# A longer pad in front of the arenas: their tiles begin at residue 64 of 512 bytes instead of 96

## The chip, the cores and the metric

The kernel runs on one core of a Trainium2 chip (trn2). The metric is the device time of one execution in microseconds; the time quoted for a kernel is the median of its runs. TensorE (PE in the profile) multiplies, with its weight loads shown apart as PEld; ScalarE is ACT, VectorE is DVE, GpSimd is POOL, and SP issues most of the DMA transfers.

## The reference: what is computed

A trunk of two layers on 256 tokens with 1024 features, in float32. Each layer is a half-step SwiGLU FFN, a token mixer, and another half-step FFN; the mixer is stick-breaking attention in layer 0 and an RG-LRU recurrent block in layer 1. Each sub-layer reads an RMS norm of x that is shifted and scaled by a vector worked out from the conditioning c, and its result is gated before it is added to x.

```python
def sublayer_input(x, g, mod_j):
    shift, scale, gate = mod_j[:, 0], mod_j[:, 1], mod_j[:, 2]
    h = rmsnorm(x, g) * (1 + scale[:, None, :]) + shift[:, None, :]
    return h, (1 + gate)[:, None, :]

def swiglu(h, w_gu, w_down):
    g, u = jnp.split(h @ w_gu, 2, axis=-1)
    return (jax.nn.silu(g) * u) @ w_down
...
    for layer in range(DEPTH):
        mod = (c_act @ mod_w[layer] + mod_b[layer]).reshape(B, N_SUB, 3, D_MODEL)
        h, g = sublayer_input(x, norm_g[layer, 0], mod[:, 0])
        x = x + MACARON_W * g * swiglu(h, ffn_w_gu[layer, 0], ffn_w_down[layer, 0])
...
    return rmsnorm(x, final_norm_g)
```

The FFN is 2816 wide, the recurrent block 1280, and the attention has 16 heads of 64.

## The kernel before

**Layout.** Features lie on the 128 partitions and the 256 tokens along the free axis, so a chunk of 128 features of x is one tile of 256 columns. Every weight matrix is cut into pieces of 128x128.

**Two halves of a number.** A float32 product is made of three matmuls in the type fp32r: each operand is split into a rounded part and the rest, and the product is weights-high times data-high, weights-high times data-low, and weights-low times data-high. The weights are split on the way in: SP loads 1 MB into a buffer `raw`, ACT copies half of it into a buffer `wh` (L519), DVE subtracts to get `wl` (L522). So one 128x128 piece of weights costs three matmuls of 256 columns, all issued at L548 in `Acc.group`. The weights are the stationary operand, loaded 128 columns at a time, and the activations are the moving operand, 256 columns of 4 bytes or 1024 bytes in each partition.

**The stages.** An FFN has an *up* stage and a *down* stage. In the up stage the moving operand is `hx`, the 8 high and 8 low chunks of the normalised input, and each of the 22 pairs of gate and up tiles takes 48 matmuls. In the down stage (`down`) the moving operand is `arenar`, the 22 high and 22 low chunks of the activated result, and it takes 22 x 8 x 3 = 528 matmuls. The attention and the recurrent block end in a `down` of 8 x 8 x 3 = 192 such matmuls from their own arena. The first two tiles of a sub-layer after the first one run on 258 columns, on `hx` tiles that hold x times the scale (`up_first`), while the norm is still being worked out.

**Where tiles lie.** Most tiles are taken one after another from a pool `const`, in the order in which the program asks for them. Three pads shift what follows: `HXPAD` ahead of `hx`, `HKPAD` ahead of `hk`, `ARPAD` at the end of the pool, after the tables of modulation values. After it comes one small tile of 32 bytes (`mhalf`), and then the arenas: at the start of each sub-layer the function `enter` closes the previous arena and opens new ones, `arenar` of fp32r and `arenaf` of float32, at the same address each time.

```python
    whr, _ = ring("wh", 7, HALF, F32R)
    wlr, _ = ring("wl", 7, HALF, F32R)
    const.tile([P, HXPAD], F32, tag="pad0", name="pad0")
    hxr, _ = ring("hx", 20, TX, F32R, pitch=320)
    const.tile([P, HKPAD], F32, tag="pad2", name="pad2")
    hkr, _ = ring("hk", 2, T, F32R)
...
    fixed("pad1", ARPAD)
```

The addresses that the built program gives to its tiles, as residues of 512 bytes within a partition, are these. All pieces of `wh` and `wl` begin at 128 (a piece is 512 bytes long). The `hx` tiles are 1280 bytes apart and begin at 64 and 320 in turn; the high part of a chunk mostly has the one and the low part the other. `hk`, a copy of the first chunk of `hx`, begins at 128. An arena is handed out in cells of 512 bytes, so every tile in it begins at one residue, which is 96.

**Two kinds of interruption.** In the up stages, the tiles numbered 2, 3, 7, 9, 11, 15 and 19 (`KICKS`) read `hk` instead of the first chunk of `hx`: the same numbers at another residue. In `down`, `kick_op` (L734) puts one bf16 matmul of 64 columns with zero weights behind the first three matmuls of a chosen chunk (`kicks`): chunk 0 in an FFN, chunk 1 in the two mixers.

**What sets the order.** The program records every operation with an estimated cost and sorts them by a list scheduler (`Program.schedule`); the instructions of each engine then run in the order found. The scheduler knows buffers by their cells and not by their addresses in bytes.

Of the kernel before, what the change touches and what calls it, by code (L numbers as in the profile page):

```python
# [32 lines left out]
NFIRST = 2  # L33
LAT0, RATE0, RATE = 950.0, 390.0, 360.0
SMALL = (0, 7)
HXPAD, HKPAD, ARPAD = 112, 16, 64
KICKS = (2, 3, 7, 9, 11, 15, 19)

OFF_NG = 0
# [1282 lines left out]
```

## Time and profile before

| | |
|---|---|
| runs | 979.4, 979.3 and 978.39 us, median 979.3 us |
| profiled execution, from its first to its last instruction (span) | 978.6 us; no other time of it is given |
| TensorE matmuls and weight loads | 8102 of each |
| VectorE busy | 799.1 us |
| ScalarE busy | 564.4 us |
| read from memory | 248.92 MB, 255 GB/s over the span |
| mean granted TensorE clock | 0.997 |

The page of the profile is a page of one execution. "Busy" is the time in which an engine had an instruction under way. Matmuls are pipelined: a row gives one 256-column matmul about 0.28 us, but the next one starts after less than half of that, so what a stage costs is read from the distance between starts, and not from the duration of one. In the view in order of time, a row stands for one or more equal instructions that follow each other: "x2" at 620.46 and the row after it at 620.68 are three matmuls, and the next three begin at 620.80. The view of stretches gives for each stretch its length, the busy time of each engine with the number of instructions that are under way in it, the granted clock, and what the DMA engines did.

### The profile page before, as it was taken

What the parts mean: (1) busy time and instruction counts of PE and PEld (TensorE: products, weight loads), DVE (VectorE), ACT (ScalarE), POOL (GpSimd) and SP (SyncE); (2) the same over time, 40 slices, a digit from 0 to 9 for tenths busy, and PEclk for the clock granted to TensorE, in tenths of its full rate; (3) what the DMA queues carried; (4) which work ended last, traced back from release to release, by engine and by line L of the source; (5) the groups of instructions that cost most, each with busy time, mean ns of one, the idle gap of its engine ahead of it and who ended that gap; (6) DMA issues with size and microseconds to landing.
All of it is one profiled execution on the core that took longest, in us unless ns stands there. A gap on an engine that the chain in (4) does not pass through costs nothing.

```text
span 978.6 us, 19751 instructions
## 1 busy us (share of the span) xinstructions
PE 960.4 (98%) x8102; PEld 948.4 (97%) x8102; DVE 799.1 (82%) x1325; ACT 564.4 (58%) x907; POOL 3.9 (0%) x16
## 2 busy tenths in 40 slices
PE   7999999999999999999999999999999999999996
PEld 5999999999999999999999999999999999999996
DVE  7999898798998999998789999835997996555443
ACT  4475544378886854454367544534879785444333
POOL 0000000000000000000000000000000000000000
PEclk9999999999999999999999999999999999999998
DMA  8999899854666489999977999855243646555521
GB/s 313 330 345 362 330 367 349 326 210 154 255 217 219 161 322 373 356 344 341 347 268 266 351 367 349 320 194 191 86 173 129 259 172 237 195 192 196 173 86 44
DMA packets 48189, 251.25 MB, mean 257 GB/s; under 512 B 5473, under 2 KB 6369, under 8 KB 28386
## 3 DMA queue, kind: packets, MB, share of 16 engines
q1 hardware_dynamic: 47378, 249.30, 69.6%
q8 instruction: 63, 1.03, 0.4%
q10 hardware_dynamic: 720, 0.69, 0.2%
q14 instruction: 28, 0.23, 0.1%
HBM read 248.92 MB, written 1.05 MB: 255 GB/s over the span
## 4 chain that ended last, share of the span: by engine, by line
PE 88%; DVE 6%; DMA 3%; ACT 2%; issue 1%; SPq 0%; DVEq 0%; ACTq 0%
PE bank L548 82%; DMA raw<-in_gu 3%; PE bank L880 2%; DVE wl L522 2%; DVE arenaf L1059 1%; PE bank L1003 1%; ACT arenaf L498 1%; PE bank L565 1%; DVE rawm L580 1%; ACT wh L519 1%; PE bank L956 1%; PE bank L981 1%; DVE arenaf L1056 0%; PE bank L624 0%; PE bank L983 0%
## 5 line engine op out<-in xcount | busy, mean ns | idle before, releaser
L548 PE MATMUL bank<-hx,wh 128*128 128x256 f32 (+1 forms) x3236 | 563.9, 279 | 4.5 <-ACT hx L498 2.9
L519 ACT ACTIVATE wh<-raw 128x1024 fp32r<-128x1024 f32 (+1 forms) x328 | 337.2, 1047 | 313.8 <-PE bank L548 221.7
L548 PEld LDWEIGHTS bank<-hx,wh 128*128 128x128 f32 x3236 | 492.8, 189 | 6.9 <-ACT hx L498 3.8
L522 DVE TENSOR_TENSOR wl<-raw,wh 128x1024 fp32r<-128x1024 f32 (+1 forms) x328 | 389.5, 1208 | 111.7 <-ACT wh L519 110.6
L548 PE MATMUL bank<-hx,wl 128*128 128x256 f32 (+1 forms) x1618 | 449.8, 278 | 0.0
L548 PEld LDWEIGHTS bank<-hx,wl 128*128 128x128 f32 x1618 | 305.5, 189 | 0.0
L548 PE MATMUL bank<-arenar,wh 128*128 128x256 f32 x1664 | 297.1, 282 | 0.0
L548 PEld LDWEIGHTS bank<-arenar,wh 128*128 128x128 f32 x1664 | 255.2, 188 | 0.1
L548 PE MATMUL bank<-arenar,wl 128*128 128x256 f32 x832 | 233.7, 281 | 0.0
L580 DVE SCALAR_TENSOR_TENSOR rawm<-rawm,cact 128x1024 f32<-128x1024 f32 x143 | 174.1, 1221 | 24.1 <-DMA rawm<-in_modw 23.4
L548 PEld LDWEIGHTS bank<-arenar,wl 128*128 128x128 f32 x832 | 156.8, 188 | 0.0
L498 ACT ACTIVATE arenar<-a 128x256 fp32r<-128x256 f32 x88 | 35.7, 407 | 8.6 <-DVE a L767 8.3
L772 DVE TENSOR_TENSOR arenar<-a,arenar 128x256 fp32r<-128x256 f32 x88 | 36.6, 419 | 0.6 <-ACT arenar L498 0.5
L767 DVE TENSOR_TENSOR a<-bank,sg 128x256 f32<-128x256 f32 x82 | 34.1, 418 | 0.5 <-ACT sg L498 0.3
L548 PE MATMUL bank<-hk,wh 128*128 128x256 f32 x156 | 31.2, 291 | 0.0
L498 ACT ACTIVATE sg<-bank 128x256 f32<-128x256 f32 x82 | 29.7, 367 | 1.4 <-PE bank L548 1.4
L498 ACT ACTIVATE hx<-x,mf 128x256 fp32r<-128x256 f32 x40 | 18.8, 504 | 19.5 <-DVE x L689 19.5
L498 ACT ACTIVATE hx<-hpre,mf 128x256 fp32r<-128x256 f32 x48 | 23.5, 503 | 10.8 <-DVE hpre L650 8.2
L689 DVE SCALAR_TENSOR_TENSOR x<-bank,mf,x 128x256 f32<-128x256 f32 x48 | 21.7, 479 | 9.8 <-PE bank L548 9.6
L548 PEld LDWEIGHTS bank<-hk,wh 128*128 128x128 f32 x156 | 24.0, 189 | 0.5
L880 PE MATMUL bank<-wh,hx 128*128 128x256 f32 x128 | 23.4, 280 | 0.0
L652 DVE SCALAR_TENSOR_TENSOR hx<-hpre,mf,hx 128x256 fp32r<-128x256 f32 x48 | 23.0, 480 | 0.5 <-ACT hx L498 0.5
(109 smaller groups left out, 541.6 us busy)
## 6 DMA issues: line engine op xcount, KB each, us to landing
raw<-in_gu SPq DMA_DIRECT2D x79, 1024.0 KB, 6.0
rawm<-in_modw SPq DMA_DIRECT2D x144, 512.0 KB, 6.7
raw<-in_wdn SPq DMA_DIRECT2D x44, 1024.0 KB, 6.4
raw<-in_win SPq DMA_DIRECT2D x10, 1024.0 KB, 4.9
raw<-in_qk SPq DMA_DIRECT2D x8, 1024.0 KB, 4.9
raw<-in_gu SPq DMA_DIRECT2D x14, 512.0 KB, 7.5
raw<-in_wout SPq DMA_DIRECT2D x5, 1024.0 KB, 5.2
raw<-in_wv SPq DMA_DIRECT2D x4, 1024.0 KB, 6.6
```

The costliest lines, as they stand in the source:

```text
L498: act.activation(o(), i(), f, **{k: (v() if callable(v) else v) for k, v in kw.items()})
L519: act.activation(h()[:, :m], raw()[:, a : a + m], AF.Copy)
L522: dve.tensor_tensor(lo()[:, :m], raw()[:, a : a + m], f32(h()[:, :m]), ALU.subtract)
L548: pe.matmul(o(b()), wc(u()), xc(v()), start=start and n == 0, stop=stop and n == len(passes) - 1, skip_group_check=True)
L565: pr.op("PE", c_mm(n, 4), lambda: pe.matmul(o(b()), wc(w()), xc(x32()), start=start, stop=stop, skip_group_check=True), [w, x32] + ([] if ...
L580: dve.scalar_tensor_tensor(raw(), raw(), 1.0, cact(), ALU.mult, ALU.mult, accum_out=m()[:, t : t + 1])
L652: V(lambda: dve.scalar_tensor_tensor(lo()[:, :T], hp(), sh()[:, c], f32(hi()[:, :T]), ALU.add, ALU.subtract), T, [hp, (sh, d), hi], [lo], ...
L689: dve.scalar_tensor_tensor(x[d](), acc.b()[:, j * T : (j + 1) * T], gate()[:, d : d + 1], x[d](), ALU.mult, ALU.add)
L767: V(lambda: dve.tensor_tensor(a(), b()[:, T:], sg(), ALU.mult), T, [(b, (1, 0)), sg], [a])
L772: V(lambda: dve.tensor_tensor(y[1](), a(), f32(y[0]()), ALU.subtract), n, [a, y[0]], [y[1]])
L880: pe.matmul(o, u()[:, tb * P : (tb + 1) * P], v()[:, c0 : c0 + 256], start=start and n == 0, stop=k == KD - 1 and n == 2, skip_group_check ...
L956: pe.matmul(zb[e]()[:, BL[i]], v()[rows, kc], w()[rows, qc], start=False, stop=i == 1 and n == 2, skip_group_check=True)
```

## The change

One number changes. The pad tile `pad1` is 184 floats long instead of 64, so 736 bytes of each partition instead of 256. `mhalf` and all arenas move up by 480 bytes; the arenas begin at residue 64 of 512 bytes instead of 96, and `mhalf` at 32 instead of 64. Nothing else moves: `raw`, `wh`, `wl`, `hx`, `hk`, x and all the tables keep their addresses. The instructions and their order are the same on every engine in both programs (5497 rows on TensorE, 1122 on VectorE, 853 on ScalarE, 20 on GpSimd and 323 on SyncE, row by row); only addresses within them differ.

```diff
-HXPAD, HKPAD, ARPAD = 112, 16, 64
+HXPAD, HKPAD, ARPAD = 112, 16, 184
```

## The prediction, made before the changed kernel ran

> **What bounds the kernel now.** The first view is the page: the busy row, the granted clock by slices and the engine shares of the chain that ended last.
>
> ```profile
> span 978.6 us, 19751 instructions
> PE 960.4 (98%) x8102; PEld 948.4 (97%) x8102; DVE 799.1 (82%) x1325; ACT 564.4 (58%) x907; POOL 3.9 (0%) x16
> ...
> PEclk9999999999999999999999999999999999999998
> ...
> PE 88%; DVE 6%; DMA 3%; ACT 2%; issue 1%; SPq 0%; DVEq 0%; ACTq 0%
> ```
>
> TensorE is under way for 98% of the span at full clock, and 88% of the chain runs through it. So the second question is whether it waits inside its stages. The view of waits, TensorE alone, gives in its longest row (microseconds in total, times, longest)
>
> ```profile
> PE bank L548 <- ACT hx L498: 2.9, 2, 2.6
> ```
>
> and the others are shorter still. For most of the span the kernel therefore lasts as long as its matmuls take one after the other, and a nanosecond on the distance between starts counts in full. The third view, the groups of instructions with their shapes apart, says how many matmuls read the arenas.
>
> ```profile
> L548 PE MATMUL bank<-hx,wh 128*128 128x256 f32 x2916 | 504.6, 278 | 4.5 <-ACT hx L498 2.9 <-DVE hx L652 1.4
> ...
> L548 PE MATMUL bank<-arenar,wh 128*128 128x256 f32 x1664 | 297.1, 282 | 0.0
> ...
> L548 PE MATMUL bank<-arenar,wl 128*128 128x256 f32 x832 | 233.7, 281 | 0.0
> ```
>
> 1664 + 832 = 2496 matmuls take an arena tile as moving operand: 4 x 528 in the FFNs' down stages and 2 x 192 in the mixers'. They stand beside 2916 and more on `hx` of the same shape, with weights in the same buffers at the same residue, 128. What differs is the residue of the moving tile: 96 for the arenas, 64 and 320 for `hx`.
>
> The fourth view, the order of time on TensorE, compares the distances. Below are the first and the last row of three pieces of 17 threes (51 matmuls) each, and nothing else runs on TensorE between them.
>
> ```profile
> 620.46 0.39 PE L548 MATMUL bank<-hx,wh 128*128 128x256 f32 x2
> ...
> 626.24 0.39 PE L548 MATMUL bank<-hx,wh 128*128 128x256 f32 x2
> ```
>
> ```profile
> 59.78 0.40 PE L548 MATMUL bank<-hx,wh 128*128 128x256 f32 x2
> ...
> 65.79 0.40 PE L548 MATMUL bank<-hx,wh 128*128 128x256 f32 x2
> ```
>
> ```profile
> 659.00 0.40 PE L548 MATMUL bank<-arenar,wh 128*128 128x256 f32 x2
> ...
> 665.03 0.40 PE L548 MATMUL bank<-arenar,wh 128*128 128x256 f32 x2
> ```
>
> 5.78, 6.01 and 6.03 us, so 113.3, 117.8 and 118.2 ns per matmul. The reader is to see two things. The same instruction on `hx` runs at two paces, and keeps to either for tens of matmuls; I call them the **fast lock** (113.3) and the **slow lock** (117.8). And the arenas at residue 96 run at neither but slightly behind the slow one. That this holds for whole stages is shown by the view of stretches, from the matmul behind the bf16 one of L734 to the end of each FFN's down stage, with the recurrent block's as fourth row:
>
> ```profile
> core 0: us, PE busy (x) PEld busy (x) DVE busy (x) ACT busy (x) POOL busy (x), PEclk, DMA share, GB/s
> ...
> 141.69:203.90 62.21, 62.21 (x527) 62.21 (x527) 52.39 (x85) 26.93 (x43) 0.00 (x0) 1.00 0.90 336
> 443.56:505.78 62.22, 62.22 (x528) 62.22 (x527) 50.71 (x81) 25.80 (x36) 0.00 (x0) 1.00 0.94 340
> 627.31:689.53 62.22, 62.22 (x529) 62.22 (x527) 31.61 (x43) 26.15 (x36) 0.00 (x0) 1.00 0.53 185
> 762.01:784.47 22.46, 22.46 (x193) 22.46 (x192) 21.42 (x42) 15.91 (x32) 0.00 (x0) 1.00 0.65 249
> 905.96:968.17 62.21, 62.21 (x527) 62.21 (x527) 24.89 (x30) 23.32 (x32) 0.00 (x0) 1.00 0.30 102
> ```
>
> 62.2 us for the 525 matmuls that are left in each (2 to 4 more are still under way at the edges), 118.5 ns each with the 0.09 us that the L734 matmul costs its successor. It is the same at 94% and at 30% DMA share, so it isn't traffic; the arena stages have one pace of their own.
>
> **The change, part by part.**
>
> *Matmuls that read the arenas as moving operand.* After the change their tiles begin at 64 with weights still at 128, which is what two of three matmuls on `hx` have (the middle one reads the low part, at 320, 256 bytes further). So the trace shows their pace: one of the two locks. By the fast one each saves (6.03 - 5.78) / 51 = 4.9 ns. Which lock is the open point. The first of the three pieces is the end of an up stage, 0.7 us ahead of its down stage, so `down` is entered in the fast lock, but then L734 interrupts the stream after three matmuls and the lock is drawn again. Here are four such draws on `hx` at 64: a short stall at 58.92, a longer one at 52.96, a restart behind L956 at 287.60, and at 70.39 six matmuls on `hk`.
>
> ```profile
> 58.92 0.55 PE L548 MATMUL bank<-hx,wh 128*128 128x256 f32 x2
> ...
> 59.43 0.40 PE L548 MATMUL bank<-hx,wh 128*128 128x256 f32 x2
> ```
>
> ```profile
> 53.83 0.39 PE L548 MATMUL bank<-hx,wh 128*128 128x256 f32 x2
> ...
> 54.16 0.39 PE L548 MATMUL bank<-hx,wh 128*128 128x256 f32 x2
> ```
>
> ```profile
> 288.05 0.39 PE L548 MATMUL bank<-hx,wh 128*128 128x256 f32 x2
> ...
> 288.38 0.39 PE L548 MATMUL bank<-hx,wh 128*128 128x256 f32 x2
> ```
>
> ```profile
> 70.39 0.40 PE L548 MATMUL bank<-hk,wh 128*128 128x256 f32 x2
> ...
> 71.81 0.39 PE L548 MATMUL bank<-hx,wh 128*128 128x256 f32 x2
> ...
> 73.17 0.39 PE L548 MATMUL bank<-hx,wh 128*128 128x256 f32 x2
> ```
>
> The first falls into the slow lock (0.35 to 0.36 us for three, as the piece from 59.78 goes on), the second and third into the fast one (0.33 to 0.34), the fourth leaves the slow for the fast (four threes in 1.36 us). The fast is the likelier outcome. What L734 does to a stream at 64 no row shows; the nearest row is its present effect on a stream at 96:
>
> ```profile
> 627.27 0.20 PE L734 MATMUL bank<-ident,zero 128*128 128x64 bf16 x1
> 627.31 0.49 PE L548 MATMUL bank<-arenar,wh 128*128 128x256 f32 x2
> ...
> 627.75 0.40 PE L548 MATMUL bank<-arenar,wh 128*128 128x256 f32 x2
> ```
>
> One long first matmul (0.49 us for two against 0.40), like a restart after a stall. So I take the restarts' odds, two of three for the fast lock, raised a little because the entry is in it. All four FFN stages meet L734 in the same position behind the same three matmuls, so they fall alike.
>
> The sum for the fast lock: FFNs 4 x 525 x 4.9 ns = 10.3 us; recurrent block 189 x 4.9 = 0.9 us; attention, whose 192 are cut into pieces by other products, some two thirds in the fast lock, 0.6 us. Together **11.8 us**, less some 8 matmuls of settling per stage, 6 x 8 x 4.9 ns = 0.2 us: **11.6 us**.
>
> *Matmuls that read an arena in another way.* Scores, sums and values of the attention have both operands in the arena or weights elsewhere, and the 72 single-pass pieces on float32 read `arenaf`. The pitch between moving and weight tiles inside one arena stays, so I take nothing; the bound, 4.9 ns on some 300 such instructions either way, is 1.5 us, and half of that lies beside ScalarE and VectorE work on the chain.
>
> *Reads and writes of the arenas by ScalarE and VectorE.* The rows for 256 columns at different residues:
>
> ```profile
> L772 DVE TENSOR_TENSOR arenar<-a,arenar 128x256 fp32r<-128x256 f32 x88 | 36.6, 419 | 0.6 <-ACT arenar L498 0.5
> L498 ACT ACTIVATE arenar<-a 128x256 fp32r<-128x256 f32 x88 | 35.7, 407 | 8.6 <-DVE a L767 8.3
> ...
> L498 ACT ACTIVATE sq<-x 128x256 f32<-128x256 f32 x45 | 17.2, 406 | 2.9 <-DVE x L689 2.3 <-DVE ssq L617 0.5
> L617 DVE TENSOR_TENSOR ssq<-ssq,sq 128x256 f32<-128x256 f32 x40 | 16.8, 421 | 2.6 <-ACT sq L498 1.4
> ```
>
> 419 and 421, 407 and 406 ns, with the arena at 96 and `ssq` and `sq` at 128: no effect of the residue, taken as zero.
>
> *What is late next.* A down stage of 62.2 us would last 59.6 and asks for its weights and modulation tiles sooner. In the stretch from 443.56 that is 340 GB/s x 62.2 us = 21.1 MB in 59.6 us, 355 GB/s. The stretch
>
> ```profile
> 75.00:81.00 6.00, 6.00 (x56) 6.00 (x55) 6.00 (x8) 4.15 (x6) 0.00 (x0) 1.00 1.02 372
> ```
>
> shows 372, by which the load takes 56.9 us, so it still fits. If only 345 were had, it would last 61.3 us, and 1.7 us of the gain would go in this stage and about 1 us in the first, where 336 GB/s stand. I charge 0.2 us in all. The forecast is 978.6 - 11.4 = 967.2 us for the profiled execution; the median of the runs is 0.7 us above its span, so **967.9 us**.
>
> **A rule that speaks against the change.** The Trainium skill, SBUF — State Buffer, section "Who interferes with whom", has one cause of contention alone, the port pair shared by VectorE and GpSimd, and says "PE and ACT never wait on anyone"; TensorE: Matmul & The Clock Gate, "Step-by-step: what each phase is for", adds that loading the next weights takes no read bandwidth from the running matmul. By these an address can't matter, and the sum would be zero, 979.3 us. The trace doesn't bear this out as it stands: one instruction shape runs at 113.3, 117.8 and 118.2 ns with full clock and no wait.
>
> **The rivals.**
>
> *The slow lock* (nothing that can be measured). L734 leaves the stream at 117.8 ns: 2496 x 0.4 ns = 1.0 us saved, 978.3 us. For it: the draw at 58.92. Against it: the other three, and the entry in the fast lock. The case in which the residue is not the cause at all, and `hx` is faster for another reason (its order of output banks, its pitch), is as likely to end here, at 979.3.
>
> *Mixed.* The mixers or some stages keep to the slow lock: with two of four FFN stages 973 us. For it: the pieces of the attention are redrawn often. Against it: the four stages start alike. A DMA bound that gives back 2.7 us (above) ends at about 970.5.
>
> *Slower: no lock, with 64 after 64.* On `hx` the low part lies at 320; in the arena both parts lie at 64, and nothing in the trace has that. A stream of 64s that doesn't lock has a row: the `hx` matmuls of 258 columns,
>
> ```profile
> 515.88 0.28 PE L548 MATMUL bank<-hx,wl 128*128 128x258 f32 x1
> ...
> 517.69 0.28 PE L548 MATMUL bank<-hx,wl 128*128 128x258 f32 x1
> ```
>
> 15 matmuls in 1.81 us, 120.7 ns, and 119.8 ns without their two extra columns at 113.3 / 256 ns each. That is 1.6 ns above today's pace, 2496 x 1.6 = 4.0 us, **983.3 us**. It decides if the step of 256 bytes between high and low part matters; against it speaks that in the fast lock two tiles at 64 also follow each other, the third of a group and the first of the next, and the rows still come every 0.34 us.
>
> **How the numbers follow.** Fast lock in all or nearly all stages 0.68, own range 966 to 970 (all 2496 at 4.9 ns and 0.8 us for the other products below; a DMA bound of 2 us above). Mixed 0.10, 970 to 977. Slow lock or no effect 0.15, around 978.3 to 979.3. Slower 0.07. To leave out no more than 2 in 10 the range has to take in the slow lock's nearest part: 965.8 to 978.3. A measurement of this kernel can tell about 0.2% (2 us) from no change, so faster means below 977.3: 0.78; same 0.15; slower 0.07.
>
> **What would show it.** Right: threes 0.34 us apart in the four stages behind L734, stretches of 59.6 us, and the up stages unchanged at 113.3. Slow lock: threes an even 0.353 us apart. Slower: threes of uneven length above 0.355. A DMA bound would show as waits of L548 for ACT or DVE in the stages from 141 and 443. The prediction is wrong if L734 starts a stream at 64 in the slow lock, or if the pace is set by something other than the moving tile's residue.

## The result, and the profile after

| | before | changed kernel | ratio, 95% interval |
|---|---|---|---|
| first comparison | 979.35 us (978.39 to 979.92, 4 runs) | 970.06 us (968.3 to 973.06, 4 runs) | 0.9913 (0.989 to 0.9937) |
| repeated later (experiment 5) | 979.02 us (977.7 to 980.01, 7 runs) | 967.38 us (967.06 to 967.7, 4 runs) | 0.9883 (0.9868 to 0.9898) |

The kernel became faster by 9.3 us, and by 11.6 us when it was measured again; the forecast was 967.9 us. The execution profiled in the first comparison is the longest of its four, 973.06 us with a span of 971.4 us, so its trace shows both the gain and where part of it went.

The page of this execution, with the busy row and the chain that ended last:

```profile
span 971.4 us, 19751 instructions
PE 951.9 (98%) x8102; PEld 938.5 (97%) x8102; DVE 797.0 (82%) x1325; ACT 562.7 (58%) x907; POOL 3.8 (0%) x16
...
PE 79%; DVE 8%; DMA 8%; ACT 3%; issue 2%; SPq 0%; DVEq 0%; ACTq 0%
```

The counts are those of before, and TensorE is still under way for 98% of the span, with 8.5 us less. But its share of the chain fell from 88% to 79%, and that of DMA rose from 3% to 8%, that of VectorE from 6% to 8%: somewhere in this execution they end last. First the gain. The groups of instructions with their shapes apart show the matmuls on the arenas and the two writers of an arena:

```profile
L548 PE MATMUL bank<-arenar,wh 128*128 128x256 f32 x1664 | 285.0, 277 | 0.0
...
L548 PE MATMUL bank<-arenar,wl 128*128 128x256 f32 x832 | 229.7, 276 | 0.0
L772 DVE TENSOR_TENSOR arenar<-a,arenar 128x256 fp32r<-128x256 f32 x88 | 36.5, 419 | 0.6 <-ACT arenar L498 0.5
L498 ACT ACTIVATE arenar<-a 128x256 fp32r<-128x256 f32 x88 | 35.5, 405 | 8.6 <-DVE a L767 8.4
```

The writers take 419 and 405 ns, as they did at 96 (419 and 407), so for them no effect of the residue can be seen. The matmuls' own durations fell by 5 ns (282 to 277, 281 to 276). What counts is the distance between starts, in the view in order of time behind L734 in the down stage of 626 us; the second fence row is the first long matmul, the last is 17 threes behind the row above it:

```profile
626.31 0.20 PE L734 MATMUL bank<-ident,zero 128*128 128x64 bf16 x1
626.35 0.49 PE L548 MATMUL bank<-arenar,wh 128*128 128x256 f32 x2
...
626.80 0.39 PE L548 MATMUL bank<-arenar,wh 128*128 128x256 f32 x2
...
632.58 0.39 PE L548 MATMUL bank<-arenar,wh 128*128 128x256 f32 x2
```

51 matmuls in 5.78 us, 113.3 ns each: the fast lock, and it is there from 626.80 us on, the second three behind L734. The view of stretches gives whole stages; the columns are the stretch, its length, each engine's busy time with the number of instructions, the granted clock, the DMA share and GB/s. The first row runs to the first down stage's L734, the fourth and fifth are the down stage from 442 and the 154 matmuls that follow it, which end within the second tile of 256 columns of the next up stage.

```profile
core 0: us, PE busy (x) PEld busy (x) DVE busy (x) ACT busy (x) POOL busy (x), PEclk, DMA share, GB/s
0.00:143.24 143.24, 134.19 (x1068) 128.79 (x1069) 127.97 (x227) 76.78 (x118) 2.35 (x15) 0.99 0.92 338
143.24:202.84 59.60, 59.60 (x528) 59.60 (x527) 49.46 (x81) 25.35 (x40) 0.00 (x0) 1.00 0.92 346
308.74:320.66 11.92, 11.92 (x108) 11.92 (x106) 11.45 (x29) 8.32 (x23) 0.00 (x0) 1.00 0.60 198
442.13:501.73 59.60, 59.60 (x528) 59.60 (x527) 47.94 (x72) 22.99 (x29) 0.00 (x0) 1.00 0.92 342
501.73:523.08 21.35, 19.93 (x155) 18.86 (x154) 21.32 (x46) 17.70 (x33) 0.00 (x0) 1.00 0.54 197
626.35:685.96 59.61, 59.61 (x529) 59.61 (x528) 31.72 (x46) 26.03 (x36) 0.00 (x0) 1.00 0.55 199
758.40:779.92 21.52, 21.52 (x192) 21.52 (x192) 21.10 (x42) 15.70 (x32) 0.00 (x0) 1.00 0.67 256
901.39:960.99 59.60, 59.60 (x528) 59.60 (x527) 24.88 (x30) 23.19 (x32) 0.00 (x0) 1.00 0.30 107
```

Three rows of the same view of the kernel before, for the stretches that the prediction doesn't show (the start, the longest piece of the attention's `down`, and the stretch behind the down stage from 443):

```profile
0.00:141.69 141.69, 132.51 (x1069) 127.18 (x1069) 126.84 (x226) 77.75 (x118) 2.35 (x15) 1.00 0.92 340
309.63:322.04 12.41, 12.41 (x107) 12.41 (x106) 11.90 (x31) 8.81 (x23) 0.00 (x0) 1.00 0.50 173
505.78:524.02 18.24, 18.24 (x154) 18.19 (x153) 18.20 (x37) 15.32 (x26) 0.00 (x0) 1.00 0.47 175
```

The account follows. The four FFN down stages went from 248.86 us together (62.21 + 62.22 + 62.22 + 62.21) to 238.41, which is 10.45; the recurrent block gave 0.94 (22.46 to 21.52), and the attention's longest piece 0.49. That is 11.9 us. Two stretches are longer: the start by 1.55 us (141.69 to 143.24), and the stretch behind the down stage from 442 by 3.11 us (18.24 to 21.35). 11.9 - 1.55 - 3.11 = 7.2, and the spans differ by 978.6 - 971.4 = 7.2 us. The rest of the span is as long as before to 0.02 us, but by parts that cancel: the stretch behind the first down stage, up to the first matmul of L880, also grew by 0.4 us (12.04 to 12.46), and the attention's shorter pieces and small gains elsewhere won as much back.

What stands in the 3.11 us is shown by the chain of the stretch from 480 to 525 us alone (start, length, what):

```profile
485.28 9.81 DMA rawm<-in_modw
...
496.35 2.27 DVE wl L522 x2
498.62 0.79 DVE x L689 x2
...
499.49 1.14 DVE rawm L580 x2
500.63 0.40 DVE hx L642
501.02 0.40 DVE x L689
501.42 0.39 DVE hx L642
```

One modulation tile takes 9.81 us, where the median of this execution is 6.8 us, and L580, which multiplies it, waits for it on VectorE. Behind it in VectorE's order stand two weight splits, the residual additions (L689) and the scaled chunks (L642) that the next stage's first matmuls read. TensorE is done with its down stage at 501.73 and catches up with L642 two chunks later; the view in order of time shows its two longest stalls there:

```profile
507.15 0.39 PE L548 MATMUL bank<-hx,wh 128*128 128x258 f32 x1 [0.38 <-DVE hx L642]
...
509.68 0.48 PE L624 MATMUL bank<-ssq,ones 128*128 128x256 f32 x1 [0.94 <-DVE ssq L617]
```

So the stage itself kept its pace, and a late transfer was paid for behind it. That this is a matter of the faster stage asking for its data sooner (**lost slack**) is one reading; that it is the chance of these four runs is the other. Experiments 5 to 8 bear on that. Experiments 1 to 3 ask what it is in an address that sets the pace, and experiment 4 what L734 does to it.

### The profile page after: what moved, and what is told of

It reads as the page before. It is cut to its first block, busy times and chain, and to the rows that moved or that the text cites. A ratio compares the mean times of both kernels' runs of the same rounds, so it can differ in the third digit from the quotient of the medians.

```text
span 971.4 us, 19751 instructions
## 1 busy us (share of the span) xinstructions
PE 951.9 (98%) x8102; PEld 938.5 (97%) x8102; DVE 797.0 (82%) x1325; ACT 562.7 (58%) x907; POOL 3.8 (0%) x16
## 4 chain that ended last, share of the span: by engine, by line
PE 79%; DVE 8%; DMA 8%; ACT 3%; issue 2%; SPq 0%; DVEq 0%; ACTq 0%
PE bank L548 73%; DMA rawm<-in_modw 4%; DMA raw<-in_gu 3%; DVE wl L522 3%; PE bank L880 2%; DVE arenaf L1059 1%; DVE rawm L580 1%; PE bank L1003 1%; ACT arenaf L498 1%; ACT wh L519 1%; PE bank L565 1%; PE bank L956 1%; PE bank L981 1%; DMA x<-in_xT 1%; DVE hpre L650 0%
## 5 line engine op out<-in xcount | busy, mean ns | idle before, releaser
L548 PE MATMUL bank<-hx,wh 128*128 128x256 f32 (+1 forms) x3236 | 566.8, 279 | 5.0 <-ACT hx L498 3.4
L548 PEld LDWEIGHTS bank<-hx,wh 128*128 128x128 f32 x3236 | 494.7, 189 | 8.4 <-ACT hx L498 4.3
L548 PE MATMUL bank<-hx,wl 128*128 128x256 f32 (+1 forms) x1618 | 450.4, 278 | 0.0
L548 PEld LDWEIGHTS bank<-hx,wl 128*128 128x128 f32 x1618 | 306.6, 190 | 0.0
L548 PE MATMUL bank<-arenar,wh 128*128 128x256 f32 x1664 | 285.0, 277 | 0.0
L548 PEld LDWEIGHTS bank<-arenar,wh 128*128 128x128 f32 x1664 | 250.7, 188 | 0.1
L548 PE MATMUL bank<-arenar,wl 128*128 128x256 f32 x832 | 229.7, 276 | 0.0
L580 DVE SCALAR_TENSOR_TENSOR rawm<-rawm,cact 128x1024 f32<-128x1024 f32 x143 | 174.1, 1221 | 30.4 <-DMA rawm<-in_modw 29.7
L548 PEld LDWEIGHTS bank<-arenar,wl 128*128 128x128 f32 x832 | 156.2, 188 | 0.0
L548 PE MATMUL bank<-hk,wh 128*128 128x256 f32 x156 | 31.2, 291 | 0.0
L689 DVE SCALAR_TENSOR_TENSOR x<-bank,mf,x 128x256 f32<-128x256 f32 x48 | 21.6, 478 | 7.8 <-PE bank L548 7.7
L548 PEld LDWEIGHTS bank<-hk,wh 128*128 128x128 f32 x156 | 24.0, 189 | 0.5
L880 PE MATMUL bank<-wh,hx 128*128 128x256 f32 x128 | 23.5, 281 | 0.0
```

The source lines that it names most:

```text
L548: pe.matmul(o(b()), wc(u()), xc(v()), start=start and n == 0, stop=stop and n == len(passes) - 1, skip_group_check=True)
L580: dve.scalar_tensor_tensor(raw(), raw(), 1.0, cact(), ALU.mult, ALU.mult, accum_out=m()[:, t : t + 1])
L689: dve.scalar_tensor_tensor(x[d](), acc.b()[:, j * T : (j + 1) * T], gate()[:, d : d + 1], x[d](), ALU.mult, ALU.add)
L880: pe.matmul(o, u()[:, tb * P : (tb + 1) * P], v()[:, c0 : c0 + 256], start=start and n == 0, stop=k == KD - 1 and n == 2, skip_group_check ...
```

## The experiments

**1 and 2: one residue for each down stage.** From the changed kernel, the pad goes back to 64 floats, and each arena gets a pad of its own when `enter` opens it. So one run shows four FFN stages at four residues. Attention and recurrent block lie at 64 in experiment 1 and at 320 in experiment 2, whose `SHIFT` is (24, 56, 32, 56, 56, 48).

```diff
-HXPAD, HKPAD, ARPAD = 112, 16, 184
+HXPAD, HKPAD, ARPAD = 112, 16, 64
+SHIFT = (104, 120, 112, 8, 120, 16)
...
         pl = st.enter_context(tc.tile_pool(name=f"ph{k}", bufs=1, reuse_waits="tile"))
+        if SHIFT[k]:
+            pl.tile([P, SHIFT[k]], F32, name=f"shift{k}")
```

A shift of s floats puts the arena at 96 + 4s, modulo 512: in experiment 1 the FFNs' at 0, 32, 128 and 160, in experiment 2 at 192, 224, 320 and 288, in order of time.

> The pad ahead of the arenas is that of before (residue 96), and each sub-layer's arena gets a small pad of its own: the four FFN arenas begin at residues 0, 32, 128 and 160 of 512, the two mixers' at 64. Read by the stretch behind L734 of each FFN's down stage (525 matmuls: 62.2 us before, 59.6 us after the change). Theory of the moving tile's residue (its distance from the weights' residue, 128, decides whether the stream can lock at 113.3 ns): none of the four is at 64 or 320, so all four stretches last 61.8 us or more, and the recurrent block's stage, at 64, runs at 113.3 ns. Rival, that 96 was merely a bad place (a tile that straddles 64-byte blocks): 0 and 128 run at 113.3 ns (59.6 us), 32 and 160 at 118 or worse.

> As the run before, with the FFN arenas at residues 192, 224, 320 and 288, and the mixers' at 320. Theory of the residue with a period of 256 bytes (hx holds its low parts at 320 and its high parts at 64, and both run at 113.3): 320 gives 59.6 us, 288 gives 62.2 us as 32 would, 192 and 224 61.8 us or more. Rival, a period of 512 bytes or only the pair 64: 320 gives about 62. Rival, multiples of 64 bytes are good: 192 and 320 give 59.6, 224 and 288 about 62.

Measured, one run each: 975.96 and 973.52 us, beside 979.4 us (978.58 to 981.21, 7 runs) for the kernel before on the same chip. The stretches of experiment 1, each from behind L734 to the end of the down stage (the fourth row is the recurrent block):

```profile
139.81:202.19 62.38, 62.38 (x528) 62.38 (x527) 51.82 (x85) 26.89 (x43) 0.00 (x0) 1.00 0.88 333
440.86:502.55 61.69, 61.69 (x529) 61.69 (x527) 51.30 (x80) 26.41 (x37) 0.00 (x0) 1.00 0.91 340
624.03:687.11 63.08, 63.08 (x529) 63.08 (x528) 31.64 (x43) 26.13 (x36) 0.00 (x0) 1.00 0.53 187
759.56:781.08 21.52, 21.52 (x193) 21.52 (x191) 21.09 (x42) 15.70 (x32) 0.00 (x0) 1.00 0.67 257
902.56:963.89 61.33, 61.33 (x528) 61.33 (x527) 24.89 (x30) 23.25 (x32) 0.00 (x0) 1.00 0.29 104
```

And those of experiment 2:

```profile
139.53:201.45 61.92, 61.92 (x529) 61.92 (x527) 50.49 (x82) 26.50 (x43) 0.00 (x0) 1.00 0.90 329
440.16:503.24 63.08, 63.08 (x528) 63.08 (x527) 51.60 (x83) 26.44 (x37) 0.00 (x0) 1.00 0.91 337
624.75:684.35 59.60, 59.60 (x529) 59.60 (x527) 31.39 (x43) 26.03 (x36) 0.00 (x0) 1.00 0.53 194
756.77:778.29 21.52, 21.52 (x192) 21.52 (x191) 21.09 (x42) 15.70 (x32) 0.00 (x0) 1.00 0.68 258
899.78:961.47 61.69, 61.69 (x528) 61.69 (x528) 24.89 (x30) 23.27 (x32) 0.00 (x0) 1.00 0.29 103
```

In the table the pace is the stretch, less 0.1 us for the first matmul behind L734, over 525. The distance is the moving tile's residue less that of the weights (128), modulo 256.

| arena at | distance | stretch, us | ns per matmul |
|---|---|---|---|
| 64 (change), 320 | 192 | 59.60 | 113.3 |
| 160 | 32 | 61.33 | 116.6 |
| 32, 288 | 160 | 61.69 | 117.3 |
| 192 | 64 | 61.92 | 117.8 |
| 96 (before) | 224 | 62.22 | 118.3 |
| 0 | 128 | 62.38 | 118.6 |
| 128 | 0 | 63.08 | 120.0 |
| 224 | 96 | 63.08 | 120.0 |

Every stage runs at full granted clock (1.00), and has TensorE under way throughout; 61.69 us stand at 340 GB/s in the one run and at 103 in the other. So the address of the moving tile alone is worth up to 63.08 - 59.60 = 3.5 us in a stage. Residues 256 bytes apart give the same stretch, 64 and 320 as well as 32 and 288. And nothing near 64 shares its gain: 32 is at 117.3, 96 at 118.3. It is neither a matter of a larger alignment (0 and 128 are among the slowest) nor a slope. Two stages of experiment 1 came out below the 61.8 us that were expected of all four (61.69 at 32, 61.33 at 160), and 288 at 61.69 instead of 62.2: away from 64 there is not one slow pace but several. Most distances were seen in one stage of one execution (160 in two, 224 in four); whether another distance than 192 has two paces isn't known.

**3: the weights moved too.** If the residue itself matters, the moving tile has to be at 64; if the distance to the weights does, any place will serve that is 64 bytes below theirs. A pad of 32 bytes ahead of everything moves all tiles of the changed kernel by 32: weights at 160, `hx` at 96 and 352, arenas at 96, which is where they were before.

```diff
+    const.tile([P, 8], F32, tag="pad3", name="pad3")
     rawr, _ = ring("raw", 3, CH)
```

> The changed kernel with a pad of 32 bytes ahead of every tile: weights at 160, hx at 96 and 352, hk at 160, arenas at 96. If the distance between moving tile and weights decides (minus 64 in 256), nothing is lost: down stretches 59.6 us and up stages at 113.3 ns, total within 2 us of the changed kernel. If the moving tile's own residue decides, both the up and the down stages fall to about 118 ns: 4854 up matmuls by 4.9 ns and 2496 by 4.9 ns, some 36 us slower than the changed kernel, about 1005 us.

Measured, one run: 965.47 us. Two of its four down stages in the view of stretches; the other two are 59.61 and 59.60 us:

```profile
139.44:199.04 59.60, 59.60 (x528) 59.60 (x527) 50.03 (x82) 26.21 (x42) 0.00 (x0) 1.00 0.91 342
437.69:497.29 59.60, 59.60 (x528) 59.60 (x527) 51.03 (x82) 26.31 (x36) 0.00 (x0) 1.00 0.93 352
```

Arenas at 96, which took 62.2 us with weights at 128, take 59.6 with weights at 160. So residue 96 is not slow and 64 not fast in themselves; what the change did was to bring the moving tile to 64 bytes below the weights, modulo 256. (In experiment 3 all tiles moved, so that it is the weights which count is inferred: they are the only other operand that these matmuls read, and the pace is the same in stages with 342 and with 107 GB/s of other traffic.) It was tried at this one distance; whether the other rows of the table move with the weights in the same way was not tried.

**4: no interruption in `down`.** The forecast had L734 draw the lock anew. Here `kick_op` is left out of `down`, which takes away matmuls with zero weights.

```diff
-                        if d == 0 and k == 2 * c and c in kicks:
-                            kick_op(*place[d])
```

> The changed kernel without the bf16 matmul of L734 in the down stages (its weights are zero, so the values stay). My step was that the matmul draws the lock again and that the entry is already in the fast lock: then without it the four FFN stages stay at 113.3 ns from their first matmul and each is about 0.13 us shorter (its 0.04 us and the 0.09 us it costs the next), total 0.5 us less or the same. Rival, that it is what brings the stream at 64 into the fast lock: without it the stages run at 117.8 ns and the kernel is some 10 us slower, about 979.

Measured: 968.93 us (967.99 to 969.99, 4 runs), 0.9892 of the kernel before (0.9874 to 0.991). Two of its down stages, now from their first matmul, with 528 in each stretch (the other two are the same, 59.84 us):

```profile
142.41:202.25 59.84, 59.84 (x531) 59.84 (x530) 50.59 (x83) 26.60 (x43) 0.00 (x0) 1.00 0.93 344
896.04:955.88 59.84, 59.84 (x530) 59.84 (x529) 24.90 (x31) 23.45 (x32) 0.00 (x0) 1.00 0.30 106
```

59.84 / 528 = 113.3 ns from the first matmul on. In an FFN the stream comes out of the up stage in the fast lock (its threes are 0.34 us apart up to the end, in all four) and stays in it, and nothing needs to be drawn. With L734 the same 528 took 59.99 us (in the stage of the changed kernel from its first one, which starts at 625.97 us, to the end at 685.96), so the interruption costs 0.15 us in a stage and 0.6 us in four, too little to be seen in the times.

The recurrent block is another matter. Ahead of its stage stand the 32 single-pass matmuls of L565, and not a stream in the fast lock. These are its 192 matmuls, from the first, in experiment 4 and in experiment 8 (below), both without L734:

```profile
752.99:774.95 21.96, 21.96 (x194) 21.93 (x193) 21.57 (x42) 16.26 (x33) 0.00 (x0) 1.00 0.69 263
753.16:775.96 22.80, 22.80 (x194) 22.77 (x193) 21.97 (x42) 16.32 (x33) 0.00 (x0) 1.00 0.66 255
```

The addresses are the same, and so is the clock, but the second is 0.84 us longer: its 17 threes from 753.70 to 759.71 us take 6.01 us, 117.8 ns per matmul, the slow lock. With L734 and the arena at distance 192, all 7 recurrent blocks and all 21 FFN stages in the traces of this case are fast behind it. Whether L734 is what makes the recurrent block fast, two traces without it can't say.

**5 to 8: is the missing gain lost slack?** The changed kernel itself, in more rounds (5); the same with fewer modulation tiles in the down stage where the late one stood, 8 multiplications of L580 in it in place of 18, and more in the next FFN (6); the kernel of experiment 3 again (7); experiments 6 and 4 together (8). All four ran on one chip, another than that of experiments 1 to 4, and are compared with the same runs of the kernel before. The edit of 6 and 8:

```diff
-    rate = {0: (1.5, SQ, 30), 1: (1.5, 0, 9), 2: (1.3, 0, 32), 3: (1.3, 0, 32)}
+    rate = {0: (1.5, SQ, 30), 1: (1.5, 0, 9), 2: (0.4, 0, 32), 3: (1.6, 0, 40)}
```

> The changed kernel itself, for its spread. The four runs known lie from 968.3 to 973.06 us, and the profiled one, the longest, loses 3.1 us where VectorE waits for modulation tiles at the end of the third down stage and 1.5 us in the loads before the first down stage. Theory of lost slack (the faster down stages run the transfers so near their limit that a late modulation tile now stops TensorE in some runs): the runs keep a spread of 3 us or more and a median of 969 to 970.5. Rival, chance in the first runs: median 967.5 to 968.5 and a spread of 2 us, as before.

> The changed kernel with the modulation tiles spread otherwise: rate of the third FFN-like sub-layer's hook (layer 0, second FFN) 0.4 instead of 1.3, and 1.6 in the next one. By the order of VectorE 36 of them are then worked off in that sub-layer instead of 48, and 43 instead of 31 in the next, whose down stage moved only 199 GB/s. Theory of lost slack: the stall behind the third down stage is gone from every run, median 0.5 to 2 us below the changed kernel's and the spread narrower. Rival, that the lost time comes from the loads at the start alone: the same as the changed kernel within 0.5 us.

> Every tile 32 bytes further on, with the arenas still 64 bytes behind the weights in 256. Its one run gave 965.47 us with a start 3.8 us shorter than the changed kernel's profiled one. If that was chance of the start, its median is the changed kernel's within 1 us; if an address itself matters to the transfers (the raw buffers at 160 instead of 128), it stays 2 us or more below it.

> Both edits at once: fewer modulation tiles in the third sub-layer and no bf16 matmul in the down stages. If both help on their own (0.5 to 1 us from the matmul, 0.5 to 2 from the tiles), 966 to 968 us; if neither does, the changed kernel's median.

| | median (lowest to highest, 4 runs), us | ratio to before (95%) | span, us |
|---|---|---|---|
| 5: changed kernel | 967.38 (967.06 to 967.7) | 0.9883 (0.9868 to 0.9898) | 965.5 |
| 6: fewer modulation tiles | 967.17 (966.22 to 967.97) | 0.9881 (0.9866 to 0.9895) | 966.2 |
| 7: all moved by 32 bytes | 967.34 (966.21 to 968.65) | 0.9887 (0.9871 to 0.9904) | 964.5 |
| 8: fewer tiles, no L734 | 967.72 (966.55 to 968.69) | 0.9886 (0.9871 to 0.9901) | 967.0 |

The start, the down stage from 440 and the stretch behind it in experiment 5:

```profile
0.00:141.33 141.33, 132.19 (x1068) 126.32 (x1069) 127.78 (x227) 76.97 (x118) 2.35 (x15) 1.00 0.93 343
439.58:499.19 59.61, 59.61 (x529) 59.61 (x527) 51.27 (x81) 25.62 (x36) 0.00 (x0) 1.00 0.95 357
499.19:517.38 18.19, 18.19 (x154) 18.14 (x153) 18.16 (x37) 15.25 (x26) 0.00 (x0) 1.00 0.48 176
```

and the last two of them in experiment 6:

```profile
440.45:500.06 59.61, 59.61 (x529) 59.61 (x527) 39.07 (x56) 25.95 (x35) 0.00 (x0) 1.00 0.68 248
500.06:518.25 18.19, 18.19 (x154) 18.14 (x153) 17.89 (x33) 15.62 (x25) 0.00 (x0) 1.00 0.65 232
```

In experiment 5 the same program has the stretch behind the stage at 18.19 us and TensorE under way all through it; the load came at 357 GB/s. Experiment 6 takes the load down to 248 GB/s and gains nothing: 967.17 against 967.38 us, with intervals that overlap. So the theory of lost slack falls as an account of the median: the stage fits its data into 59.6 us, and the four runs of experiment 5 lie within 0.7 us. The four kernels can't be told apart, and none beats the changed one by more than the measurement shows. By experiment 7 the 965.47 us of experiment 3 were a good run, and no gain of its addresses.

What stays of it: the margin is thin. Seven traces have their FFN down stages in the fast lock, the one after and those of experiments 3 to 8, and three of them lose time behind such a stage. Beside the first execution these are experiment 7, behind the stage from 437,

```profile
437.56:497.16 59.60, 59.60 (x528) 59.60 (x527) 51.09 (x81) 24.63 (x33) 0.00 (x0) 1.00 0.96 362
497.16:516.15 18.99, 18.92 (x155) 18.50 (x153) 18.96 (x40) 15.92 (x29) 0.00 (x0) 1.00 0.49 175
```

and experiment 8, behind the first down stage. Here this stretch, up to the first matmul of the attention's L880 (L878 in experiment 8), is shown for experiment 5 and then for experiment 8:

```profile
200.94:212.91 11.97, 11.97 (x100) 11.92 (x99) 11.76 (x29) 10.71 (x22) 0.00 (x0) 1.00 0.61 220
201.17:214.29 13.12, 12.55 (x100) 12.09 (x99) 12.95 (x31) 11.67 (x25) 0.00 (x0) 1.00 0.60 204
```

That is 0.8 us lost in experiment 7 and 1.15 in experiment 8, against 3.11 and 0.4 in the first execution. In experiment 8 L548 waits for L642 again, 0.6 us, behind a stage that experiment 6's edit leaves as it was. The profiled run of experiment 8 (968.69 us) is the longest of its four, and this stall and the slow recurrent block make 2 us of it. The traces of the kernel before and of experiments 1 and 2, whose FFN down stages from 140 and 440 us are slower, show no such stall; with three traces against seven that is a hint and no proof of lost slack. Why a modulation tile took 9.81 us once is not settled; nor is why the first four runs as a group, 968.3 to 973.06 us, lie above all four of experiment 5, since only one of them left a trace and the chip that they ran on is not on record.

## Why the prediction was right, point by point

**The bound.** TensorE's own pace set the time of the down stages. Their distance between starts fell by 5.0 ns and the time with it, at 0.30 as at 0.92 DMA share.

**The lock that would be drawn.** Fast, in all four FFN stages and in the recurrent block, as forecast. The sum had 10.3 us for the FFNs, and 10.45 were measured; 0.9 for the recurrent block, and 0.94 were; 0.6 for the attention, whose six pieces on the arena gave 0.70 together (23.24 to 22.54 us). In experiment 5 all that lies between the first down stage and the end of the attention's last piece is 0.96 us shorter than before (118.14 to 117.18), so the other products there, put at nothing, gave 0.2 to 0.3 us more.

Two of the reasons don't hold as they were given. The first is the draw: the forecast took L734 for a new draw with odds of two in three. In the FFNs there is nothing to draw, since by experiment 4 the entry in the fast lock is enough, and 28 fast stages out of 28 behind L734 give no sign of a draw. The second is the residue. The forecast said that it would be wrong if the pace were set by something other than the moving tile's residue, and by experiment 3 it is: it is the distance to the weights that counts. "The pace that `hx` has at 64" was the right number because the weights stay at 128, which the prediction named only in passing; had the change moved the weights too, its reason would have failed.

**What is late next.** Charged 0.2 us, with a bound of 1.7 us in the stage from 443 and about 1 us in the first. It was said to show as waits of L548 inside the stages. In the first profiled execution it came to 3.1 us and stood behind the stage, in the 258-column tiles that wait for VectorE; the bound had counted the bytes of the stage, and not what stands behind one late tile in VectorE's order. In the trace of experiment 5 it was nothing, and the stage took its data at 357 GB/s, where 355 had been worked out; in those of experiments 7 and 8 it was about 1 us. The start's 1.5 us lies ahead of all but the first three matmuls on an arena, and varies from run to run: the first down stage is reached at 143.24 and 141.33 us in two executions of the changed kernel, and at 139.4 to 142.4 us in experiments 1 to 4.

**From span to time.** The 0.7 us were too little: the profiled execution of the first comparison has 973.06 us with a span of 971.4, that of experiment 5 967.3 with 965.5, so 1.7 to 1.8 us. The forecast of the span, 967.2 us, was too long by as much (965.5 in experiment 5), and the two errors cancel in 967.9. By the same 1.7 us the profiled execution of the kernel before took about 980.3 us, 1 us more than the median of 979.3, so its span was a high base to start from. That the forecast lies within 0.6 us of 967.38 is in this part luck. By medians the gain is 979.02 - 967.38 = 11.6 us, against 11.4 forecast.

**The rivals.** The slow lock and no effect fell for the FFNs: none of their stages at distance 192 runs at 117.8 ns. "64 after 64" fell too, since the arenas have both parts at 64 and run at 113.3 ns. The mixed case holds in two small places. The recurrent block of experiment 8, without L734, took the slow lock and lost 0.84 us. And in the trace after and in those of all eight experiments, a piece of 36 matmuls in the attention, with the arena at distance 192 each time, ran at the slow lock's 117.8 ns; 36 x 4.5 ns make 0.16 us.

**The rule that spoke against it.** The Trainium skill, SBUF — State Buffer, "Who interferes with whom", by which TensorE never waits on anyone, would, as the prediction read it, have made every row of the table above the same. The measurement decides: 113.3 to 120.0 ns by address alone, with clock and operands' shapes unchanged. No run here shows that TensorE waits for another engine in these rows, so what falls is that reading and not the sentence.

## What to carry to other kernels

Where a stage is bound by matmuls, measure the distance between their starts (not their durations), and compare stages of the same shape: a difference of a few per cent at full clock and without waits can be a matter of where the two operands lie. Then try addresses: a pad that differs from stage to stage tries several in one run, and the residue that counts here is that of the moving tile relative to the weights, modulo 256 bytes. The same addresses can have two paces, so look at more than one stage before a residue is called fast or slow. And before a late transfer in one trace is called the price of a gain, run the same program again.

## What the runs showed of the hardware that was not expected

The pace of equal fp32r matmuls (128x128 weights, 256 columns of 4 bytes) takes at least seven values between 113.3 and 120.0 ns, set by the distance of moving tile and weights modulo 256 bytes, and steady to a few hundredths of a microsecond over 525 matmuls. It is no monotonic function of it: 120.0 at 0 and at 96, 116.6 at 32 between them, and 113.3 only at 192 of the eight distances tried (steps of 32 bytes). At distance 192 a stream can also stay at 117.8 ns, as the kernel before shows on `hx` and experiment 8 on an arena for a whole stage of 192 matmuls; that is the value of distance 64, and whether the two have a cause in common was not tried. What in the memory or in TensorE makes the difference no run here shows.
